# Wider pieces of the experts' weights, a regrouped set of turns, a shorter last routing and a written order at the end, in a hierarchical mixture-of-experts layer

## The chip, the cores and the metric

The kernel runs on 1 core of one Trainium2 chip. The metric is the device time of one execution in microseconds, the median of several runs. A profiled execution is a single one, recorded by the hardware profiler; its span is the time between its first and its last recorded instruction, a little less than the execution's own time.

## The reference, cut to what matters

One layer of a decoder trunk for 1024 tokens of width 1024, in float32. First a mixer (an SSD group, a forgetting attention and a convolution group over one input projection, then one output projection), then a hierarchical mixture of 32 gated-MLP experts of width 512: top-1 of 4 groups, then top-2 of that group's 8 experts. The part that the change is about:

```python
x = x + g_m * y                
h = rms_norm(x, norm_ffn_g[l]) * (1.0 + sc_f) + sh_f
p_g = softmax(h @ w_rg + b_rg); g_sel = argmax(p_g)
e_logits = (h @ w_re + b_re).reshape(m, 4, 8)[g_sel]
top_p, top_i = lax.top_k(softmax(e_logits), 2)
weights = top_p / sum(top_p) * p_gsel
...
hid = silu(xb @ w_gate[e]) * (xb @ w_up[e])
ys = hid @ w_down[e]
out = zeros.at[stok].add(ys[dest] * sw)
x = x + g_f * out
return rms_norm(x, final_norm_g)
```

## The kernel before

**Stages.** The mixer runs first, in eight blocks of 128 tokens; then the output projection with the routing of each block; then the loop over the 32 experts; then the final norm. Float32 accuracy comes from a split: each operand is rounded to a high part (`hi`, made by a copy on ACT) and a remainder (`lo`, made by a subtraction on DVE), and each product is three matmuls, `xh`·`hi`, `xl`·`hi`, `xh`·`lo`.

**Early in the mixer** four tiles of the queries' and keys' weights are worked through by `qk_tile(t)`; inside that loop, after `t == 0`, a small table `ncu` is transposed by PE (L487) and stored.

**Routing.** For each block of 128 tokens, `post_steps` (from L1008) makes the normed tokens `h2` and the router's logits `L`; the logits are made feature-major (`wrp` stationary, `xT` moving), copied by ACT to `rT`, transposed back (L1023) and added up in two operations (L1024, L1025). `h2` of the last block is scaled in one operation over 1024 columns (L1033) and written to `h2_d` in DRAM. `route_steps` (from L1057) makes one-hot rows, positions (L1118 to L1121), the table `tab` of each expert's tokens (matmuls L1131, addition L1135) and from it, in three operations (L1137 to L1139), the integer indices `toki`. `gather(e)` (L1308) is an indirect DMA by GpSimd that fetches the 128 rows of expert `e` from `h2_d` into one of two buffers `xg`, `xq`.

**The experts' weights** are loaded on SP's queue in halves of a matrix (128 x 2048, 1 MB; 6 halves an expert, 192 in all) by `load_half` (issue at L1198). `halves` holds NHALF = 18 buffers, carved by `room` out of the mixer's tiles as these die; 15 are loaded before the routing ends, and POST = 3 are held back and loaded after `gather(0)`, by way of a GpSimd memset behind it. `after_load` lets at most DEPTH = 5 loads run at once (DC = 2 for the first NC_ = 15, DL = 3 for the small ones at the end). `order` is the sequence of the matrices: `(e, 0)` gate, `(e, 1)` up, then `(e-1, 2)` down of the expert before.

**The expert loop.** `xpose(e)` transposes the gathered rows (8 transposes L1318 into two PSUM banks, each split into `xh`, `xl` at L127, L128). `gate_or_up` works through a matrix in four pieces of 1024 columns; `piece` (L1328) casts one on ACT (`phi`) and takes the remainder on DVE (`plo`), three buffers of each. The matmuls (L1340 to L1342) follow in groups of three. `hidden` (L1346 to L1348) is silu on ACT and a product on DVE. `turn_hidden` (4 transposes, L1354) turns it, inside the first matrix of the next expert; `down` (L1368 to L1370) follows `up` of the next expert, and in its middle the tokens of the expert after are transposed and the next gather is issued (`next_tokens`). The result is scaled on DVE (L1374) and scattered with addition into `x1_d` in DRAM (L1378, GpSimd). `row_spread` (L1282) spreads a row of 1024 numbers over the partitions with eight matmuls; it is run for `gf` ahead of the first expert, for `fng` within the last.

**The end.** The eight blocks of `x1_d` are loaded back; `norm_of` (L1292 to L1296) squares a block on ACT, takes the power on GpSimd and scales on DVE. Six blocks (FB) are normed without the last expert's rows, whose 128 tokens are fetched apart into `xr`, added up on GpSimd (L1483), normed and scattered into the output at the end (L1485). For the other two blocks PE adds the last expert's rows with a one-hot matrix (L1470 to L1472).

**The order on each engine** is made by a planner from costs. Instructions that go through `tc.keep_in_program_order` stay in the order in which they are written relative to each other.

The pieces of `gate_or_up` and the step of the loop over the experts read:

```python
            for q in range(4):
                if q == QT and then:
                    then()
                hi, lo = piece(e, m, q)
...
            if e < NE - 1:
                hid = hidden(pg, gate_or_up(e, 1, xh, xl))
                load_next()
                if e:
                    down(e - 1, *hts[e - 1], lambda: next_tokens(e + 1))
```

## Time and profile before

| | us |
|---|---|
| median of 3 runs | 1276.93 (1276.75 to 1277.41) |
| the profiled execution, its own time | 1275.77 |
| its span | 1273.9 |
| PE busy (matmuls) | 1186.6 (93% of the span) |
| PE weight loads busy | 928.3 (73%) |
| DVE busy | 980.5 (77%) |
| ACT busy | 736.4 (58%) |
| GpSimd busy | 268.2 (21%) |
| moved by DMA | 313.21 MB, mean 246 GB/s |

PE, DVE, ACT, POOL and SP are TensorE, VectorE, ScalarE, GpSimd and SyncE; PE's weight loads overlap with its matmuls. A busy share over the whole span is a mean of stages that differ: the loop over the experts takes some 597 of the 1274 us (649.88 to 1246.70), and there the engines stand at other shares than in the mixer before it. The granted clock of PE is a share of full speed (1.00 is 2.4 GHz, 0.50 is 1.2 GHz); its mean over the span is 0.972. A row of the timeline gives the start of an instruction, its duration and, in brackets, for how long its engine had been idle and whose end it waited for; neighbouring instructions of one kind stand in one row, with their number behind the x.

### The profile page before, as it was taken

The numbers are of one execution on the slowest core, as the hardware profiler recorded it, in microseconds if no ns is written. First come the engines' busy times: TensorE is split into PE (matmuls) and PEld (weight loads), VectorE is DVE, ScalarE is ACT, GpSimd is POOL, SyncE is SP. The second block draws the span as 40 slices with busy tenths as digits, with TensorE's granted clock in tenths as the row PEclk, the third lists the DMA queues.
The fourth block names the chain that finished last, engine by engine and source line by source line (L and its number), as shares of the span: only waits on it lengthen the run. The fifth ranks groups of instructions, "written<-read, shape, count | busy, mean of one in ns | idle before, by whom it ended". The sixth has DMA issues, their size and how long they took to land. (4 is left out here: it accounts for less than half of the span.)

```text
span 1273.9 us, 17238 instructions
## 1 busy us (share of the span) xinstructions
PE 1186.6 (93%) x6079; PEld 928.3 (73%) x6079; DVE 980.5 (77%) x1395; ACT 736.4 (58%) x1145; POOL 268.2 (21%) x200
## 2 busy tenths in 40 slices
PE   6999989999999779999779999999999999999993
PEld 4676757868678568778568877777877787787772
DVE  4789992145265676575559999999999999999985
ACT  4323322343354656563258877777877787777763
POOL 3110313100100353432111221122112212211112
PEclk9999999999999989999879999999999999999997
DMA  9316667633201553734889999999999999999726
GB/s 361 140 42 220 210 196 224 160 108 89 78 17 59 148 155 100 262 98 183 304 305 343 361 356 372 366 354 367 369 359 372 356 358 387 363 381 366 236 53 257
DMA packets 93339, 313.21 MB, mean 246 GB/s; under 512 B 23894, under 2 KB 34310, under 8 KB 70976
## 3 DMA queue, kind: packets, MB, share of 16 engines
q1 hardware_dynamic: 60750, 256.25, 54.8%
q10 hardware_dynamic: 14242, 32.51, 7.4%
q0 software_dynamic: 18256, 23.30, 7.2%
q8 instruction: 49, 0.80, 0.3%
q14 instruction: 42, 0.34, 0.1%
HBM read 289.22 MB, written 39.88 MB: 258 GB/s over the span
## 5 line engine op out<-in xcount | busy, mean ns | idle before, releaser
L1342 PE MATMUL ps_gu<-plo,xh 128*128 128x512 f32 x512 | 209.1, 408 | 9.1 <-DVE plo L1328 9.0
L1340 PE MATMUL ps_gu<-phi,xh 128*128 128x512 f32 x512 | 203.3, 397 | 1.4 <-ACT xh L127 1.4
L1328 DVE TENSOR_TENSOR plo<-wx,phi 128x1024 fp32r<-128x1024 f32 x166 | 198.1, 1220 | 7.8 <-ACT phi L1328 5.5
L1328 ACT CAST phi<-wx 128x1024 fp32r<-128x1024 f32 x166 | 173.1, 1054 | 50.7 <-PE ps_gu L1341 40.8
L1341 PE MATMUL ps_gu<-phi,xl 128*128 128x512 f32 x512 | 200.8, 392 | 0.0
L1378 POOL DMA_INDIRECT x_d<-early,toki x31 | 74.9, 2416 | 400.7 <-DVE early L1374 386.0
L1328 ACT CAST phi<-w 128x1024 fp32r<-128x1024 f32 x110 | 115.3, 1050 | 60.4 <-PE ps_gu L1341 53.1
L1328 DVE TENSOR_TENSOR plo<-w,phi 128x1024 fp32r<-128x1024 f32 x110 | 130.7, 1220 | 7.2 <-ACT phi L1328 6.3
L1342 PEld LDWEIGHTS ps_gu<-plo,xh 128*128 128x128 f32 x512 | 96.3, 188 | 40.2 <-DVE plo L1328 20.8
L1340 PEld LDWEIGHTS ps_gu<-phi,xh 128*128 128x128 f32 x512 | 96.5, 189 | 20.2 <-ACT xh L127 1.8
L1341 PEld LDWEIGHTS ps_gu<-phi,xl 128*128 128x128 f32 x512 | 96.5, 188 | 19.6
L1368 PE MATMUL ps_d<-phi,hh 128*128 128x512 f32 x256 | 100.4, 393 | 0.7 <-ACT hh L127 0.7
L1369 PE MATMUL ps_d<-phi,hl 128*128 128x512 f32 x256 | 100.5, 393 | 0.0
L1370 PE MATMUL ps_d<-plo,hh 128*128 128x512 f32 x256 | 96.4, 393 | 0.0
L182 PE MATMUL ps_pr<-h_hi,whi 128*128 128x512 f32 x224 | 91.5, 409 | 0.0
L184 PE MATMUL ps_pr<-h_hi,wlo 128*128 128x512 f32 x224 | 88.8, 396 | 1.3 <-POOL wlo L128 1.3
L183 PE MATMUL ps_pr<-h_lo,whi 128*128 128x512 f32 x224 | 89.2, 398 | 0.0
L225 DVE SCALAR_TENSOR_TENSOR cy<-u_t,cmw,cy 128x1024 f32<-128x1024 f32 x60 | 86.4, 1440 | 2.3 <-ACT cy L222 1.4
L128 POOL TENSOR_TENSOR wlo<-wraw,whi 128x1024 fp32r<-128x1024 f32 x14 | 40.0, 2866 | 161.1 <-ACT whi L127 142.9
L1328 DVE TENSOR_TENSOR plo<-cy,phi 128x1024 fp32r<-128x1024 f32 x44 | 53.8, 1222 | 6.0 <-ACT phi L1328 5.2
L994 PE MATMUL ps_wo<-wo_hi,yh 128*128 128x512 f32 x128 | 55.1, 431 | 2.1 <-ACT yh L127 2.1
L1368 PEld LDWEIGHTS ps_d<-phi,hh 128*128 128x128 f32 x256 | 48.3, 189 | 10.9 <-ACT hh L127 0.9
(405 smaller groups left out, 2570.9 us busy)
## 6 DMA issues: line engine op xcount, KB each, us to landing
w<-in_w_gu_dram SPq DMA_DIRECT2D x54, 1024.0 KB
wx<-in_w_gu_dram SPq DMA_DIRECT2D x50, 1024.0 KB
wx<-in_w_dn_dram SPq DMA_DIRECT2D x30, 1024.0 KB
at<-in_ada_r_dram ACTq DMA_DIRECT2D x64, 256.0 KB
cy<-in_w_gu_dram SPq DMA_DIRECT2D x11, 1024.0 KB
wy<-in_w_gu_dram SPq DMA_DIRECT2D x22, 512.0 KB
wy<-in_w_dn_dram SPq DMA_DIRECT2D x20, 512.0 KB
xq<-in_w_dn_dram SPq DMA_DIRECT2D x10, 1024.0 KB
```

Of the source, the lines that this page charges most:

```text
L182: PE.matmul(ps, hi[:, kt, :], h_hi[hf][:, kt, :], start=(kt == 0), stop=False)
L183: PE.matmul(ps, hi[:, kt, :], h_lo[hf][:, kt, :], start=False, stop=False)
L184: PE.matmul(ps, lo[:, kt, :], h_hi[hf][:, kt, :], start=False, stop=(kt == KT - 1))
L225: yield lambda t=t, k=k: V.scalar_tensor_tensor(cy[:, :, t], v128(u_t[:, t, k:k + T]), cmw[:, t, k:k + 1], cy[:, :, t], op0=ALU.mult, op1= ...
L1328: last[:] = [S.copy(hi, raw).ins, V.tensor_tensor(lo, raw, hi.bitcast(F32), op=ALU.subtract).ins]
L1340: PE.matmul(ps, xh[:, kt], hi[:, ks], start=(kt == 0), stop=False)
L1341: PE.matmul(ps, xl[:, kt], hi[:, ks], start=False, stop=False)
L1342: PE.matmul(ps, xh[:, kt], lo[:, ks], start=False, stop=(kt == KT - 1))
L1368: PE.matmul(pd[n], hh[:, f], hi[:, ns], start=(f == 0), stop=False)
L1369: PE.matmul(pd[n], hl[:, f], hi[:, ns], start=False, stop=False)
L1370: PE.matmul(pd[n], hh[:, f], lo[:, ns], start=False, stop=(f == 3))
L1378: G.indirect_dma_start(x1_d[:, :], bass.IndirectOffsetOnAxis(ap=toki[:, e:e + 1], axis=0), yo[:, :], None, bounds_check=T - 1, oob_is_err= ...
```

## The change

- **Early transpose.** `ncu` is transposed after the second weight tile (`t == 1`) instead of the first, and its place on PE is written.
- **Last routing.** For the last block, 8 matmuls with `xT` stationary make the logits token-major, in one operation on DVE without copy and transpose; `h2` is made and written to DRAM in halves, the second half behind the sum of the one-hot rows. The token numbers are written as `token - T`, and T is added to `tab` early, so that the last addition gives `toki` directly. The operations for the two choices of a token are ordered in pairs.
- **Loads.** NHALF = 17 instead of 18 (the tile `w2` falls away); POST = 6 instead of 3 loads are held, by a dependency on `gather(0)` instead of memsets; NC_ = 11.
- **PE during the first gather.** 25 matmuls on the identity (the ones of the kernel's start) are placed behind `gather(0)`.
- **Pieces.** Casts and remainders are made for 2048 columns at a time (two buffers of each instead of three of half the size). The matmuls of a piece run all on `hi` first, then all on `lo`; all of the experts' matmuls and transposes keep the written order.
- **Turns.** In the middle of `down(e-1)` stand `next_tokens(e+1)` and then `turn_hidden(e)`; expert 1 keeps it inside its first matrix. The turned hidden rows alternate between two tiles. `gf` is spread in the middle of expert 1, `fng` in that of expert 30.
- **Last expert.** `down(30)` and its loads come before the matrices of expert 31.
- **The end** is written out: squares of the six blocks on ACT, four scalings on DVE ahead of the last result, then the split, the addition for `xr` on DVE instead of GpSimd, and the rest; the last two blocks are stored in halves.

The diff, cut:

```diff
-NHALF = 18
+NHALF = 17
-POST = 3
+POST = 6
-QD = 1
-DC, NC_ = 2, 15
+DC, NC_ = 2, 11
-QT = 1
...
-        if t == 0:
+        if t == 1:
-            PE.transpose(pc[:32, 0:P], ncu.rearrange("p h b -> p (h b)"), ident)
+            pin(PE.transpose(pc[:32, 0:P], ncu.rearrange("p h b -> p (h b)"), ident))
...
+            if b == NB - 1:
+                pin(add)
+                pin(V.tensor_tensor(h2[:, qs_], xb[:, qs_], ccn["af"][:, qs_], op=ALU.mult))
...
+            for kt in range(KT):
+                PE.matmul(pr[:, 0:36], xT[:, kt], ccn["wrp"][:, kt, 0:36], start=(kt == 0), stop=(kt == KT - 1))
+            def half_h2(q):
+                hs = slice(512 * q, 512 * (q + 1))
+                pin(V.scalar_tensor_tensor(h2[:, hs], h2[:, hs], s2[:, 3:4], ccn["shf"][:, hs], op0=ALU.mult, op1=ALU.add))
+                S.dma_start(h2_d[bs, hs], h2[:, hs])
+            half_h2(0)
+            pin(V.scalar_tensor_tensor(L[:, b], pr[:, 0:36], s2[:, 3:4], ccn["rbias"], op0=ALU.mult, op1=ALU.add))
...
+        if lastb:
+            pin(so)
+            last_half[0](1)
...
-        if lastb:
-            V.tensor_scalar(tf, tab, 0.0, 8192.0, op0=ALU.is_equal, op1=ALU.mult)
-            V.scalar_tensor_tensor(tf, tab, -1.0, tf, op0=ALU.add, op1=ALU.add)
-            tk.append(V.tensor_copy(toki, tf).ins)
+            tk.append(pin(V.tensor_tensor(toki, pq_[:, 0:NE], tab, op=ALU.add)).ins)
...
-        order += [(e, 0), (e, 1), (e - 1, 2)] if e < NE - 1 else [(e, 0), (e - 1, 2), (e, 1)]
+        order += [(e, 0), (e, 1), (e - 1, 2)] if e < NE - 1 else [(e - 1, 2), (e, 0), (e, 1)]
...
-            room(ew.tile([P, 2048], F32, name="w2"))
...
+            hi = ex.tile([P, 2048], F32R, tag="phi", name="phi", bufs=2)
+            lo = ex.tile([P, 2048], F32R, tag="plo", name="plo", bufs=2)
...
+                for hi, lo, n in pieces(e, m, s):
+                    for k in range(n):
+                        ks = slice(512 * k, 512 * (k + 1))
+                        pin(PE.matmul(ps, xh[:, k0 + k], hi[:, ks], start=(k0 + k == 0), stop=False))
+                        pin(PE.matmul(ps, xl[:, k0 + k], hi[:, ks], start=False, stop=False))
+                    for k in range(n):
+                        ks = slice(512 * k, 512 * (k + 1))
+                        pin(PE.matmul(ps, xh[:, k0 + k], lo[:, ks], start=False, stop=(k0 + k == KT - 1)))
...
         g1 = gather(0)
-        with tc.issue_after(g1.ins):
-            for h in halves[NHALF - POST:]:
-                G.memset(h[0][:, 0:1], 0.0)
+        pw = bank("ps_warm")
+        for _ in range(WARM):
+            pin(PE.matmul(pw[:, 0:P], ident, ident, start=True, stop=True))
         gather(1)
         for _ in range(POST):
-            load_half()
+            load_half(g1.ins)
...
+            def middle():
+                next_tokens(e + 1)
+                turns()
+                if e == 1:
+                    row_spread(gf, sl[0:8, :])
+                if e == NE - 2:
+                    row_spread(fng, early[0:8, D:D + P])
...
+            if e == NE - 1:
                 down(e - 1, *hts[e - 1])
                 load_next()
...
+        sqs = [square(xbs[b]) for b in range(FB)]
+        for b in range(4):
+            finish(b, sqs[b])
+            pin(V.scalar_tensor_tensor(yo_l[:, ns], pd[n], wtab[:, NE - 1:NE], gf[:, ns], op0=ALU.mult, op1=ALU.mult))
+            pin(S.copy(yh[:, ns], yo_l[:, ns]))
+            pin(V.tensor_tensor(yl[:, ns], yo_l[:, ns], yh[:, ns].bitcast(F32), op=ALU.subtract))
+        pin(V.tensor_tensor(xr, xr, yo_l, op=ALU.add))
+        sx = square(xr)
+        for b in range(4, FB):
+            finish(b, sqs[b])
...
```

## Rows read from the trace of the kernel before

**Rows 1.** Timeline of DVE, line L1348: start us, duration us, engine, line, operation
```profile
713.52 0.68 DVE L1348 TENSOR_TENSOR hid<-hid,ps_gu 128x512 f32<-128x512 f32 x1
731.42 0.68 DVE L1348 TENSOR_TENSOR hid<-hid,ps_gu 128x512 f32<-128x512 f32 x1
749.92 0.68 DVE L1348 TENSOR_TENSOR hid<-hid,ps_gu 128x512 f32<-128x512 f32 x1
...
1211.63 0.68 DVE L1348 TENSOR_TENSOR hid<-hid,ps_gu 128x512 f32<-128x512 f32 x1
```

**Rows 2.** Windows, loop: length, then PE, PEld, DVE, ACT, POOL busy; PEclk, DMA share, GB/s
```profile
800.00:900.00 100.00, 98.32 (x456) 79.67 (x455) 96.17 (x98) 78.13 (x90) 17.29 (x10) 1.00 0.99 363
```

**Rows 3.** Timeline of PE, one expert in the loop
```profile
904.53 1.04 PE L1318 MATMUL ps_xg<-ident,xq 128*128 128x128 f32 x8
905.39 0.50 PE L1342 MATMUL ps_gu<-plo,xh 128*128 128x512 f32 x1
...
906.65 0.39 PE L1341 MATMUL ps_gu<-phi,xl 128*128 128x512 f32 x1
907.38 0.50 PE L1342 MATMUL ps_gu<-plo,xh 128*128 128x512 f32 x1 [0.34 <-DVE plo L1328]
...
915.01 0.39 PE L1342 MATMUL ps_gu<-plo,xh 128*128 128x512 f32 x1
```

**Rows 4.** Waits of SP's queue, 780 to 880 us: line, cause, us in total, times, longest
```profile
SPq L1198 <- DVE plo L1328: 78.0, 36, 3.7
```

**Rows 5.** Timeline of SP's queue, two places of the loop
```profile
960.99 8.31 SPq L1198 DMA_DIRECT2D wx<-in_w_gu_dram  x4
...
1018.05 8.63 SPq L1198 DMA_DIRECT2D wx<-in_w_gu_dram  x4
```

**Rows 6.** Timeline of PE, the early transpose
```profile
175.38 0.37 PE L487 MATMUL ps_nc<-ident,ncu 128*32 128x128 f32 x1 [5.27 <-DVE ncu L481]
```

**Rows 7.** Windows, behind the early transpose
```profile
180.00:200.00 20.00, 20.00 (x95) 14.86 (x94) 11.03 (x10) 4.61 (x7) 5.55 (x2) 1.00 0.75 232
```

**Rows 8.** Timeline of DVE and GpSimd, the last routing up to the first gather
```profile
626.30 1.28 DVE L1033 SCALAR_TENSOR_TENSOR h<-h,s,shf 128x1024 f32<-128x1024 f32 x1 [0.44 <-POOL s L124]
...
627.79 0.26 DVE L1025 SCALAR_TENSOR_TENSOR L<-ps_rt,s,L 128x36 f32<-128x36 f32 x1
...
637.46 1.17 POOL L1308 DMA_INDIRECT xg<-h_d,toki  x1 [11.19 <-DMA wx<-in_w_gu_dram]
```

**Rows 9.** The tile `xg`, its 16 gathers and other transfers
```profile
DMA to landing us min/median/max: 3.8/11.9/14.0
```

**Rows 10.** Timeline of PE, from the first gather to the first expert, and the kernel's start
```profile
643.86 3.75 PE L1282 MATMUL ps_row<-sl,ident 8*128 8x128 f32 x16 [5.48 <-DMA sl<-g_rows]
647.54 1.97 PE L1318 MATMUL ps_xg<-ident,xg 128*128 128x128 f32 x8
...
649.88 0.78 PE L1340 MATMUL ps_gu<-phi,xh 128*128 128x512 f32 x1
...
9.64 8.29 PE L292 MATMUL ps_warm<-ident 128*128 128x128 f32 x50 [9.64 <-DVE ident L105]
```

**Rows 11.** Windows, PE's clock ahead of the first expert
```profile
640.00:645.00 5.00, 1.14 (x5) 1.17 (x6) 2.07 (x2) 0.00 (x0) 0.68 (x1) 0.50 0.96 308
```

**Rows 12.** Timeline of DVE, three remainders of 1024 columns in a row
```profile
1220.13 3.49 DVE L1328 TENSOR_TENSOR plo<-w,phi 128x1024 fp32r<-128x1024 f32 x3
```

**Rows 13.** Groups by line and form, DVE, 680 to 1215 us: busy us, mean ns, idle
```profile
L128 DVE TENSOR_TENSOR xl<-ps_xg,xh 128x512 fp32r<-128x512 f32 x60 | 38.5, 683 | 0.0
```

**Rows 14.** Timeline of PE, ACT and DVE, the end
```profile
1246.70 0.39 PE L1370 MATMUL ps_d<-plo,hh 128*128 128x512 f32 x1
...
1251.93 1.06 ACT L1292 ACTIVATE wx<-w 128x1024 f32<-128x1024 f32 x1 [2.01 <-DMA w<-x_d]
...
1264.20 1.28 DVE L1296 SCALAR_TENSOR_TENSOR xg<-xg,s,wx 128x1024 f32<-128x1024 f32 x1 [0.73 <-POOL s L1294]
```

**Rows 15.** Windows, the loads of the kernel's start
```profile
10.00:15.00 5.00, 5.00 (x26) 5.00 (x26) 2.80 (x7) 4.46 (x8) 2.74 (x6) 1.00 1.04 428
```

219 lines of the change are left out of this document (118 added, 101 removed).

## The prediction

> **What bounds the kernel now.** I read four views in this order: the windows by stage, the waits of PE, the timeline of one expert on PE and DVE, and SP's own waits. From 749.92 us to 1211.63 us of the span every expert takes the same time: the line that finishes an expert's hidden row stands in 26 rows there, of which the first and the last are shown, so 461.71 / 25 = 18.47 us each [rows 1]. In that stretch PE and DVE are busy 98 and 96 of 100 us, ACT 78, and the 16 DMA engines 0.99 of the time at 363 GB/s [rows 2]. Three resources stand close together, so the order in which they give out is the question.
>
> PE gives out first. Its own work per expert is 72 matmuls of 512 columns and 12 transposes. Matmuls run at 33 steps in 7.63 us, 0.231 us each (907.38 to 915.01); eight transposes run from 904.53 to 905.39, 0.107 us each [rows 3]. That is 72 x 0.231 + 12 x 0.107 = 16.6 + 1.3 = 17.9 us. The rest, 0.56 us, is a hole in each expert: the step from 906.65 to 907.38 takes 0.73 us instead of 0.23, and the row names the rounding remainder `plo` of DVE as what PE waited for [rows 3]. The early experts have no such hole: there two neighbouring rows stand 17.90 us apart (713.52, 731.42) [rows 1]. So 17.9 us is both worked out and seen.
>
> DMA is next. In the middle of the loop SP waits 78.0 of 100 us for a weight buffer to be freed by DVE [rows 4]: loads are held back by the computation. Later the same 18 half-matrices take longer to issue than three experts take to compute: 960.99 to 1018.05 is 57.06 us, against 3 x 18.47 = 55.4 [rows 5]. There DMA can't keep up, and only the lead in the buffers hides it.
>
> **The change, part by part.**
>
> *The early transpose (L487).* PE sits idle 5.27 us before it, until DVE has made `ncu` [rows 6]. Moved one weight tile later (32 x 3 matmuls, 16 steps of 0.7 us = 11 us), its input is long there. After it PE is busy 20.00 of 20 us while DVE has 9 of 20 free [rows 7], so what was behind the stall moves up and no engine is late in its place. Bounds 0 and -5.3; I take -5.
>
> *Last routing, up to the first gather.* Removed from DVE's chain: a 1.28 us operation at 626.30 in front of the logits becomes one of half the columns, -0.6 (the other half goes behind the one-hot sum, where DVE waits for PE anyway); the second addition of the logits, 0.26 us at 627.79; three operations as small between the table and the integer index, estimated at 0.2 us each; and two groups of operations on the table are interleaved, so that one such wait on a predecessor falls away, 0.3 us by estimate. Together 0.6 + 0.3 + 0.6 + 0.3 = 1.8 us on a chain that ends with the gather's issue at 637.46 [rows 8]. Added: the second half of the last block's tokens is written to DRAM later, from about 632 us, and the gather waits for it; a DMA queued then must land in 3 us. The shortest landing among the gathers into that buffer is 3.8 us after issue [rows 9], so up to 1 us may come back. Bounds 0 and -2.5; I take -1.8: gather at 635.7.
>
> *From the gather to the first expert matmul.* Now 649.88 - 637.46 = 12.4 us. PE first waits 5.48 us for a row queued behind weight loads and spends 3.75 us spreading it over partitions (643.86), then transposes (647.54) [rows 10]. The spread goes into expert 1, where it costs PE its 16 matmuls at twice that rate, +1.9 us. Six half loads are held until the gather has landed, so it has the DMA queues for itself: I take the shortest landing, 3.8 us, against 11.9 in the median [rows 9]. Transposes could start at 635.7 + 3.8 = 639.5. Added are 25 matmuls in front of them; at the kernel's start the same (the row counts 50) took 8.29 us [rows 10]. Behind the last table matmuls at about 636 they end at 644; during the idle stretch of the routing they cost nothing. Transposes therefore start between 639.5 and 644.3, the first expert matmul 0.9 us later. I take 643.0 for that matmul: 7.3 us behind the gather instead of 12.4, -5.1. The clock: it is granted at 0.50 (1.2 GHz) at 640 to 645, where PE is busy 1.14 of 5 us [rows 11], and the first expert's matmuls run slow to 653 us. With PE running through it is 2.4 GHz: the next expert's eight transposes at 1.97 against 1.04 us [rows 3, 10], and some eight matmuls, each at twice 0.231, -0.9 - 8 x 0.2 = -2.5 (bounds 0 and -3.4).
>
> *Pieces of 2048 columns, transposes together.* DVE does one remainder instead of two. Three in a row take 3.49 us [rows 12], so about 1.2 each, and half the size takes 0.683 [rows 13]; merging two 1024s saves between 0 and 2 x 0.683 - 1.22 = 0.15 us, up to 0.9 us an expert on DVE. That does not itself move PE, but it widens the margin whose lack makes the hole. Against it, PE now needs its whole 2048 cast before its first matmul, and only two such buffers exist where three of 1024 did. The pairing (eight matmuls on the cast, four on the remainder) gives DVE 8 x 0.23 = 1.8 us after the first matmul. A cast of 2048 takes about 2 us and a remainder 2.3, and a piece occupies PE 2.77 us, so both engines keep up if the planner orders their queues well. I take the period without the hole, 17.9 us, over the 26 steps that now take 18.47 (the last from 731.42 on): -0.57 x 26 = -14.8; bounds 17.6 (one switch to transposes fewer, 0.1 us, and the steps in strict sequence at 0.228) and 18.46. Fewer buffers (17 halves, not 18) only touch the lead.
>
> *The end.* PE's last expert matmul starts at 1246.70 and DVE's last operation at 1264.20, 17.5 us later [rows 14]. In between DVE does six whole-block scalings of 1.28 us, and ACT waits for blocks of `x1_d` until 1251.93 [rows 14]. With `down` of expert 30 before both matrices of expert 31, its scatter lands some 10 us earlier against the end and the blocks with it; four scalings (4 x 1.2) then fit in front of PE's end, and the addition of the last rows moves from GpSimd to DVE. Against it, the written order makes ACT square all six blocks before it copies the last rows. I take -5, bounds -9 and +3.
>
> Sum against the profiled execution's own 1275.8 us: -5 - 1.8 - 5.1 - 2.5 + 1.9 - 14.8 - 5 = -32.3, so 1243.5. The median of the runs shown is 1.2 us above that execution; I give 1245.
>
> **A rule against it.** At 10 to 15 us the DMA engines moved 428 GB/s [rows 15], so 363 in the loop is not the top that this core can reach. The Trainium skill (HBM Reference, the table at its head and the note under it) gives about 358 GB/s as a core's share when its neighbour streams too, and about 425 alone. By the share the loop would already stand at its ceiling and win nothing; the row at 428 speaks for the other figure.
>
> **Rivals.**
>
> 1. *DMA becomes the bound.* 57.06 us for 18 halves is 3.17 us each [rows 5]. In the new kernel 181 halves (192 less the 17 - 6 loaded before) remain when the gather lands, at 639.5 - 5 = 634.5: 181 x 3.17 = 574, the last at 1208; the last six go in small transfers with three in flight, some 4 us more; cast, remainder and matmuls of the last piece 4, so PE could end at 1216, just ahead of the 1219.6 of the sum (1246.9 - 27.3). The margin is 3 us in 574: at 3.2 us a half it is gone by 2, and the blocks of `x1_d`, queued behind, add some 3; 1250. At 3.23 it would be 1255. For it: the DMA share of 0.99. Against: the rate is that of SP's issues, which the freed buffers set as well. Chance 0.25.
> 2. *The hole stays.* With two large buffers DVE may be late elsewhere, for instance when an `xl` stands behind a 2.3 us remainder. Period 18.4, and all else as summed: 1245 + 26 x 0.5 = 1258. Chance 0.15.
> 3. *Slower.* ACT and DVE run their queues in order. If the cast of the second half of `down` is put behind the three casts of the transposes, PE waits for it in every expert: those casts end about 1.6 us after the last transpose, the cast takes 2 us, so a hole of up to 3 us and a period near 20.5, 32 x 2.6 = +83. It decides from the period at which the other gains (32.3 - 14.8 = 17.5) are used up, 18.47 + 17.5/32 = 19.0 us. At 20.5 the time is 1328, at 19.6 it is 1299. Against it: the planner of the old kernel put such casts ahead. Chance 0.07.
> 4. *The routing and start bring nothing*: the 25 matmuls stand in front of the routing's own, or the gather waits for the late write. 1245 + 6.9 = 1252. Chance 0.08.
>
> The forecast itself, PE-bound with no hole, gets 0.45.
>
> **How the numbers follow.** The likeliest case gives 1245, its own range 1235 to 1255 from the bounds of start and end. The 8 in 10 range takes in rivals 1, 2 and 4 and the lower bound of the period (17.6, -8): 1231 to 1264. A difference under 0.2% (2.6 us) can't be told from none. Faster 0.91, same 0.02, slower 0.07.
>
> **What would show it.** The hidden rows of neighbouring experts 17.9 us apart (18.4 or more: rival 2; over 19.0: rival 3); no wait of PE for `plo`; ACT's casts waiting for weight loads in the last third (rival 1), with PE idle there; the early transpose without a wait; transposes of expert 0 within 9 us of the gather's issue and the clock at 2.4 GHz by then; DVE's last operation 12 to 13 us behind PE's last expert matmul. The prediction is wrong if the period is not between 17.6 and 18.2, or if the loop's weights land after 1215 us.

## The result, and the profile after

The changed kernel takes 1262.82 us (median of 4 runs, 1260.09 to 1264.04) against 1276.84 us before (1275.79 to 1277.41 in the same comparison): a ratio of 0.9888, interval 0.9873 to 0.9902. It is 14.0 us faster, where 32 were forecast. The profiled execution took 1263.57 us with a span of 1261.8 us, 12.1 us shorter than the span before. All terms below are made against that span.

The same marks were read in both traces. Some of the marks before stand in no group ahead: the last block's addition behind the output projection, and the hidden rows of experts 0 to 2 and 31. Timeline of DVE, the kernel before (start, duration, engine, line, operation, in brackets its idle time and what ended it):

```profile
622.88 0.69 DVE L1000 TENSOR_TENSOR xb<-ps_wo,xb 128x512 f32<-128x512 f32 x1 [5.34 <-PE ps_wo L996]
...
664.83 0.68 DVE L1348 TENSOR_TENSOR hid<-hid,ps_gu 128x512 f32<-128x512 f32 x1
677.81 0.68 DVE L1348 TENSOR_TENSOR hid<-hid,ps_gu 128x512 f32<-128x512 f32 x1
695.68 0.68 DVE L1348 TENSOR_TENSOR hid<-hid,ps_gu 128x512 f32<-128x512 f32 x1
...
1237.44 0.68 DVE L1348 TENSOR_TENSOR hid<-hid,ps_gu 128x512 f32<-128x512 f32 x1
```

The same view of the changed kernel, with the last block's addition, then the hidden rows of experts 0 to 2, 5, 30 and 31:

```profile
618.56 0.69 DVE L999 TENSOR_TENSOR xb<-ps_wo,xb 128x512 f32<-128x512 f32 x1 [2.97 <-PE ps_wo L995]
...
653.92 0.68 DVE L1375 TENSOR_TENSOR hid<-hid,ps_gu 128x512 f32<-128x512 f32 x1
667.23 0.68 DVE L1375 TENSOR_TENSOR hid<-hid,ps_gu 128x512 f32<-128x512 f32 x1
689.60 0.68 DVE L1375 TENSOR_TENSOR hid<-hid,ps_gu 128x512 f32<-128x512 f32 x1
...
743.65 0.68 DVE L1375 TENSOR_TENSOR hid<-hid,ps_gu 128x512 f32<-128x512 f32 x1
...
1196.85 0.68 DVE L1375 TENSOR_TENSOR hid<-hid,ps_gu 128x512 f32<-128x512 f32 x1
1224.28 0.69 DVE L1375 TENSOR_TENSOR hid<-hid,ps_gu 128x512 f32<-128x512 f32 x1
```

Each stretch is the difference of two neighbouring marks:

| stretch | before, us | after, us | difference | forecast |
|---|---|---|---|---|
| start to the last block's addition | 622.88 | 618.56 | -4.3 | -5 |
| to the first gather's issue | 14.58 | 13.04 | -1.5 | -1.8 |
| to the first expert matmul | 12.42 | 9.11 | -3.3 | -5.1 |
| to the hidden row of expert 0 | 14.95 | 13.21 | -1.7 | -2.5 |
| expert 0 to 1 | 12.98 | 13.31 | +0.3 | 0 |
| expert 1 to 2 | 17.87 | 22.37 | +4.5 | +1.9 |
| expert 2 to 30 | 515.95 | 507.25 | -8.7 | -14.8 |
| expert 30 to the end of the span | 62.27 | 64.95 | +2.7 | -5 |
| sum | 1273.9 | 1261.8 | -12.1 | -32.3 |

The front brought -10.8 of the -14.4 that were forecast. Most of what is missing lies in three rows: the loop (6.1 us), the end (7.7) and expert 1 (2.6).

**The loop.** Experts 5 to 30 take (1196.85 - 743.65) / 25 = 18.13 us each: better than 18.47 [rows 1], but not 17.9. Timeline of PE in one expert (the last `hi` matmul, the four on the remainder, the next `hi`), then DVE between the transposes and that place:

```profile
971.86 0.39 PE L1365 MATMUL ps_gu<-phi,xl 128*128 128x512 f32 x1
972.36 1.20 PE L1368 MATMUL ps_gu<-plo,xh 128*128 128x512 f32 x4
973.39 0.39 PE L1364 MATMUL ps_gu<-phi,xh 128*128 128x512 f32 x1
```

```profile
966.91 1.28 DVE L126 TENSOR_TENSOR xl<-ps_xg,xh 128x512 fp32r<-128x512 f32 x2
968.11 0.68 DVE L126 TENSOR_TENSOR hx<-ps_ht,hx 128x512 fp32r<-128x512 f32 x1
968.71 1.40 DVE L1411 SCALAR_TENSOR_TENSOR early<-ps_d,wtab,gf 128x512 f32<-128x512 f32 x2
970.02 2.28 DVE L1351 TENSOR_TENSOR plo<-w,phi 128x2048 fp32r<-128x2048 f32 x1
```

PE steps in 0.23 us, so at 972.09 it would have gone on; the remainder ends at 972.3 and PE continues at 972.36, 0.27 us late. DVE had run without a gap since 966.91, and the scaling of the expert before (L1411, 1.40 us), which PE does not wait for, stands ahead of that remainder; `xl` and `hx` do too, but PE needs these first. The waits of the weight loads name the same place 21 times in the 22 experts from 745 to 1150 us (line, cause, total, times, longest):

```profile
PEld ps_gu L1368 <- DVE plo L1351: 9.1, 21, 0.5
```

**The end.** The scatter of expert 30 and the loads of the blocks, GpSimd and SP, the kernel before:

```profile
1231.90 2.29 POOL L1378 DMA_INDIRECT x_d<-early,toki  x1 [11.11 <-DVE early L1374]
```

```profile
1238.75 0.81 SPq L1446 DMA_DIRECT2D wx<-x_d  x2
```

The changed kernel, timelines of GpSimd (the scatters of experts 29 and 30), SP, PE, ACT and DVE:

```profile
1209.32 3.35 POOL L1413 DMA_INDIRECT x_d<-early,toki  x1 [18.33 <-DVE early L1411]
1217.99 3.28 POOL L1413 DMA_INDIRECT x_d<-cy,toki  x1 [5.31 <-DVE plo L1351]
```

```profile
1225.73 4.22 SPq L1487 DMA_DIRECT2D wx<-x_d  x8
```

```profile
1230.69 0.79 PE L1400 MATMUL ps_d<-phi,hx 128*128 128x512 f32 x1 [5.01 <-ACT hx L125]
...
1238.98 0.62 PE L1403 MATMUL ps_d<-plo,hx 128*128 128x512 f32 x2
```

```profile
1229.01 1.06 ACT L1501 ACTIVATE cy<-wx 128x1024 f32<-128x1024 f32 x1 [3.72 <-DMA wx<-x_d]
...
1230.07 0.56 ACT L125 CAST hx<-ps_ht 128x512 fp32r<-128x512 f32 x1
```

```profile
1250.78 2.15 DVE L1549 SCALAR_TENSOR_TENSOR wx<-ps_ad,s,wy 128x512 f32<-128x512 f32 x3
```

The loads wait for the scatter of expert 30, and that one was issued only at 1217.99, 8.7 us behind the scatter of expert 29 into the same tensor, although DVE had its rows ready at 1214.8 (two operations from 1213.43, 1.40 us). The row puts the end of GpSimd's wait down to a remainder of DVE, which the scatter does not use; in eight further profiles the two scatters are likewise 8.5 to 9.1 us apart, and the experiment without the second one, below, shows what is waited for. The loads are asked for 1.45 us behind the last hidden row, where it was 1.31 before: no earlier. So the +2.7 us of this row of the table are 1.6 between the hidden rows of experts 30 and 31 (27.43 for 25.81), 0.1 up to the loads, and 0.9 from the loads to the end (36.07 for 35.15). Besides, ACT squares the first block, which lands at 1229, before it makes the cast `hx` that PE needs: PE stands still for 5.01 us, and its matmuls then take 0.43 us each (1.2 GHz) instead of 0.23.

**Expert 1.** The row that was moved there is spread in 16 matmuls with 8 rows of weights each:

```profile
670.63 1.15 PE L1300 MATMUL ps_row<-sl,ident 8*128 8x128 f32 x8
672.46 1.15 PE L1300 MATMUL ps_row<-sl,ident 8*128 8x128 f32 x8 [0.67 <-ACT gf L1301]
```

The spread keeps PE for 2.9 us (670.63 to 673.54), of which it waits 0.67 for ACT. Behind it the clock falls: it is 0.50 from 674 to 677 us, and the next eight matmuls take 3.29 us, not 8 x 0.23 = 1.8. Windows (length; PE, PEld, DVE, ACT, POOL busy; clock, DMA share, GB/s), first behind the first gather, where [rows 11] had 0.50, then behind the spread, then in the loop, and last behind the same spread in another run (three loads held, below):

```profile
640.00:645.00 5.00, 4.53 (x22) 3.37 (x21) 1.29 (x2) 2.72 (x3) 0.98 (x1) 1.00 1.01 425
672.00:677.00 5.00, 4.54 (x17) 3.73 (x18) 3.69 (x8) 0.99 (x2) 1.61 (x1) 0.69 1.02 416
800.00:900.00 100.00, 99.58 (x467) 80.87 (x466) 94.61 (x72) 74.70 (x61) 34.40 (x12) 1.00 0.98 370
675.00:680.00 5.00, 5.00 (x25) 4.08 (x24) 4.25 (x10) 2.50 (x2) 0.49 (x2) 1.00 0.89 362
```

In that last run the clock stays at 1.00 behind the spread, and expert 1 to 2 takes 20.77 us: 2.9 more than the 17.87 before, the spread alone. The remaining 1.6 of the 4.5 us are the clock.

**The start.** The operation that gives the integer indices `toki`, DVE, the kernel before, then the changed kernel:

```profile
636.98 0.18 DVE L1139 CAST toki<-tf 128x32 int32<-128x32 f32 x1
```

```profile
629.69 0.19 DVE L1157 TENSOR_TENSOR toki<-ps_tab,tab 128x32 int32<-128x32 f32 x1 [0.42 <-PE ps_tab L1150]
```

It ends 14.28 us behind the last block's addition before (637.16) and 11.32 after (629.88): the chain to the indices got 3.0 us shorter. The gather was issued 0.3 us behind it before, and is now issued 1.7 us behind it. GpSimd's first gather, and the warming matmuls and transposes of PE:

```profile
631.60 1.17 POOL L1325 DMA_INDIRECT xg<-h_d,toki  x1 [10.51 <-DMA h_d<-h]
```

```profile
631.84 7.76 PE L1421 MATMUL ps_warm<-ident 128*128 128x128 f32 x48
639.43 1.04 PE L1335 MATMUL ps_xg<-ident,xg 128*128 128x128 f32 x8
640.71 0.49 PE L1364 MATMUL ps_gu<-phi,xh 128*128 128x512 f32 x1 [0.24 <-ACT xh L125]
```

The gather waits for the late half of the tokens, which takes 1.4 of the 3.0 us back. The transposes begin when the 25 matmuls end. The held loads, which wait for this gather to land, are issued from 635.92 us on, so its rows were there 4.3 us behind its issue, and 3.5 us before the transposes.

### The profile page after: what moved, and what is told of

The parts are those of the page before. It is cut to its first block, busy times and chain, and to the rows that moved or that the text cites. A ratio compares the mean times of both kernels' runs of the same rounds, so it can differ in the third digit from the quotient of the medians.

```text
span 1261.8 us, 16662 instructions
## 1 busy us (share of the span) xinstructions
PE 1191.5 (94%) x6128; PEld 938.4 (74%) x6128; DVE 959.9 (76%) x1219; ACT 709.8 (56%) x976; POOL 337.0 (27%) x204
## 4 chain that ended last, share of the span: by engine, by line
PE 73%; DVE 9%; DMA 7%; issue 4%; ACT 4%; POOL 2%; SPq 0%; POOLq 0%; ACTq 0%; DVEq 0%
PE ps_gu L1368 8%; PE ps_gu L1365 7%; PE ps_gu L1364 7%; DVE plo L1351 4%; PE ps_pr L180 4%; PE ps_d L1400 4%; PE ps_d L1401 4%; PE ps_pr L181 4%; PE ps_pr L182 4%; PE ps_d L1403 4%; PE ps_o L599 3%; PE ps_wo L993 2%; PE ps_wo L994 2%; PE ps_wo L995 2%; PE ps_xg L1335 1%
## 5 line engine op out<-in xcount | busy, mean ns | idle before, releaser
L1351 DVE TENSOR_TENSOR plo<-wx,phi 128x2048 fp32r<-128x2048 f32 x88 | 199.6, 2289 | 15.2 <-ACT phi L1351 15.1
L1351 ACT CAST phi<-wx 128x2048 fp32r<-128x2048 f32 x88 | 168.0, 1909 | 71.6 <-PE ps_gu L1365 40.0
L1368 PE MATMUL ps_gu<-plo,xh 128*128 128x512 f32 x512 | 142.7, 396 | 1.3
L1351 DVE TENSOR_TENSOR plo<-w,phi 128x2048 fp32r<-128x2048 f32 (+1 forms) x48 | 107.3, 2245 | 12.1 <-ACT phi L1351 12.0
L1368 PEld LDWEIGHTS ps_gu<-plo,xh 128*128 128x128 f32 x512 | 94.1, 188 | 30.0 <-DVE plo L1351 11.5
L1365 PEld LDWEIGHTS ps_gu<-phi,xl 128*128 128x128 f32 x512 | 96.2, 188 | 25.0 <-DVE xl L126 3.5
L1351 ACT CAST phi<-w 128x2048 fp32r<-128x2048 f32 (+1 forms) x48 | 89.7, 1872 | 41.3 <-PE ps_gu L1365 23.0
L1400 PE MATMUL ps_d<-phi,hx 128*128 128x512 f32 x256 | 106.3, 415 | 5.0 <-ACT hx L125 5.0
L1401 PE MATMUL ps_d<-phi,hx 128*128 128x512 f32 x256 | 103.4, 404 | 0.0
L126 POOL TENSOR_TENSOR wlo<-wraw,whi 128x1024 fp32r<-128x1024 f32 x14 | 39.9, 2855 | 158.1 <-ACT whi L125 139.7
L1325 POOL DMA_INDIRECT xq<-h_d,toki x16 | 41.7, 2608 | 142.4 <-PE ps_xg L1335 123.7
L1325 POOL DMA_INDIRECT xg<-h_d,toki x16 | 38.6, 2414 | 152.0 <-PE ps_xg L1335 80.3
L1403 PE MATMUL ps_d<-plo,hx 128*128 128x512 f32 x256 | 72.1, 398 | 0.0
L1400 PEld LDWEIGHTS ps_d<-phi,hx 128*128 128x128 f32 x256 | 49.9, 195 | 15.7 <-ACT hx L125 5.2
## 6 DMA issues: line engine op xcount, KB each, us to landing
w<-in_w_gu_dram SPq DMA_DIRECT2D x29, 1024.0 KB, 10.3
```

The source lines that it names most:

```text
L1351: last[:] = [S.copy(hi[:, cs], raw).ins, V.tensor_tensor(lo[:, cs], raw, hi[:, cs].bitcast(F32), op=ALU.subtract).ins]
L1365: pin(PE.matmul(ps, xl[:, k0 + k], hi[:, ks], start=False, stop=False))
L1368: pin(PE.matmul(ps, xh[:, k0 + k], lo[:, ks], start=False, stop=(k0 + k == KT - 1)))
L1400: pin(PE.matmul(pd[n], hh[:, f], hi[:, ns], start=(f == 0), stop=False))
L1401: pin(PE.matmul(pd[n], hl[:, f], hi[:, ns], start=False, stop=False))
L1403: pin(PE.matmul(pd[n], hh[:, f], lo[:, ns], start=False, stop=(f == 3)))
```

## The experiments

All are edits of the changed kernel, some on top of one another, but for one of the kernel before. A ratio is always against the kernel before on the same chip; the changed kernel stands at 0.9888.

### The loop: the order on DVE

The scaling of an expert's result and its scatter are put behind the remainders that PE needs next, for all but the last experts:

```diff
+                pcs = pieces(e, m, s)
+                if s and late_:
+                    with tc.issue_after(last[1]):
+                        late_()
...
-                down(e - 1, *hts[e - 1], middle)
+                res = down(e - 1, *hts[e - 1], middle)
```

> The changed kernel, but the two scalings of an expert's result on DVE (and its scatter) stand behind the remainder of the second half of the next gate matrix, not ahead of it. Theory A (order of DVE's queue: that remainder is late by 0.27 us in each expert because xl, xl, hx and the two scalings, 3.4 us, stand ahead of it): the period falls from 18.13 to 17.9 us and the time by 5 to 7 us. Theory B (DVE has 17.8 us of work in an expert, as much as PE, so the lateness only moves to another piece): period 18.05 or more, less than 2 us. Theory C (DMA delivers a half matrix each 3.02 us and no faster): period 18.1, PE and ACT now wait for loads.

1255.93 us, ratio 0.9831 (0.9815 to 0.9848), 6.9 us less than the changed kernel. The period from expert 5 to 28 is (1153.26 - 741.99) / 23 = 17.88 us; the waits for the remainder at L1368's place fall from 21 to 3. The hole was the order on DVE, not its load. The last two steps stay at 19.26 and 18.88 us.

Is it the DMA engines that hold those two? The same without the scatters of experts 0 to 28, whose results are then missing in the output:

```diff
+                if e >= NE - 3:
+                    G.indirect_dma_start(x1_d[:, :], bass.IndirectOffsetOnAxis(ap=toki[:, e:e + 1], axis=0), yo[:, :], None,
+                                         bounds_check=T - 1, oob_is_err=False, compute_op=ALU.add)
```

> The kernel of early_late without the scatters of the experts 0 to 28 into x1_d: their results are left out of the output, and some 1 MB of the 7.5 MB that DMA moves for an expert with them. Theory A (DMA is the bound near the end of the loop: in early_late two experts there take 19.3 and 18.9 us): these two take 17.8 to 18.0 us like the others, and SP again waits for buffers in the second half. Theory B (the two are late for another reason, in DVE's or PE's order): they stay at 19 us.

1257.56 us in a single execution. Those steps are 19.26 and 18.90 us, though the DMA share fell from 0.97 to 0.88 in the one and from 0.68 to 0.16 in the other. With the scatters SP waits for earlier loads to land in much of 850 to 950 us; without them its only wait is for buffers that DVE frees:

```profile
SPq L1217 <- DVE plo L1351: 85.8, 38, 4.2
```

PE's time is the same in both, so transfers do not set these steps: rival 1 does not hold here. In both steps DVE waits 0.9 us for a cast of ACT that stands behind those of the transposes, and ahead of these ACT is idle for 1.78 and 2.36 us. That is the order that rival 3 described, at 1.0 to 1.4 us an expert; no run moves this cast alone, so that it is the cause is not shown.

Then the size of the pieces: 1024 columns again, four buffers of each, but PE's written order, turns and all else as changed.

```diff
-            hi = ex.tile([P, 2048], F32R, tag="phi", name="phi", bufs=2)
-            lo = ex.tile([P, 2048], F32R, tag="plo", name="plo", bufs=2)
...
+            for raw in wts[e, m][s][0:2]:
+                hi = ex.tile([P, 1024], F32R, tag="phi", name="phi", bufs=4)
+                lo = ex.tile([P, 1024], F32R, tag="plo", name="plo", bufs=4)
```

> The changed kernel with casts and remainders of 1024 columns again, in four buffers of each in the place of two of 2048; a piece's matmuls still run on the cast first, then on the remainder, and all else is as changed. Theory A (the wide pieces brought the period from 18.47 to 18.13 us): the period goes back to 18.4 us and the time rises by 5 to 8 us. Theory B (the written order of PE and the turns together brought it; with half the size DVE can go on sooner and one remainder is late less): period 17.9 to 18.0 us, the time falls by 3 to 6 us.

1259.23 us, ratio 0.9858 (0.9841 to 0.9876): not slower than with wide pieces. Twenty experts in a row take 17.75 us each (725.84 to 1080.91), less than with 2048 columns. One reading is that DVE's small operations fit between shorter remainders; that was only argued. One step near the end takes 23.06 us. Timelines of DVE and PE there:

```profile
1163.10 1.41 DVE L1408 SCALAR_TENSOR_TENSOR early<-ps_d,wtab,gf 128x512 f32<-128x512 f32 x2 [2.86 <-DMA x_d<-early,toki]
```

```profile
1165.69 0.73 PE L1365 MATMUL ps_gu<-plo,xh 128*128 128x512 f32 x2 [3.27 <-DVE plo L1347]
```

DVE may not overwrite the only result buffer `early` before the scatter of the expert before has landed; behind it in DVE's queue stands the remainder that PE wants. That scatter's issue alone kept GpSimd busy for 10.27 us (from 1143.32), where the one after it takes 2.32. With a second buffer for results (and three of `plo`, which makes room for it) that must go:

```diff
-            yo = free[1] if e == NE - 2 else early[:, 0:D]
+            yo = free[1] if e == NE - 2 else yo2_ if e % 2 else early[:, 0:D]
```

> The kernel of small_pieces with two buffers in turn for the scaled result that is scattered (three buffers of 1024 for the remainders instead of four, to make room). In small_pieces 22 steps of the loop took 17.81 us each and one near its end 23.1, in which DVE's scaling waited 2.9 us for the scatter before it to leave the only buffer. Theory A (that buffer is the cause): the long step falls to 17.8 to 18.5 us, the time to 1253 to 1255. Theory B (the loads of weights have fallen behind by then and the lateness only shows there): a step of 21 us or more stays near the end.

1253.29 us, ratio 0.9832 (0.9810 to 0.9854). The long step is gone; the last five are 18.2 to 18.5 us. So the loop's gain does not come from the wide pieces, which took part of it back. What else the change made there (PE's written order, casts before remainders, the turns), and one more buffer for casts than before, were not told apart.

### The start

The early transpose alone, in the kernel before:

```diff
-        if t == 0:
+        if t == 1:
             pc = bank("ps_nc")
-            PE.transpose(pc[:32, 0:P], ncu.rearrange("p h b -> p (h b)"), ident)
+            tc.keep_in_program_order(PE.transpose(pc[:32, 0:P], ncu.rearrange("p h b -> p (h b)"), ident))
```

> The kernel before, with the early transpose moved behind the second weight tile and its place on PE written, and nothing else of the change. Theory A: the stretches behind it move up by 4.4 us, as they stand in the changed kernel's trace (addition of the last block at 622.9 becomes 618.5), and all of it reaches the end: 1272.5. Theory B: it is given back, since the expert loop waits for weights whose loads start no earlier: under 1 us.

1271.32 us, ratio 0.9954 (0.9937 to 0.9970): -5.5 us. The last block's addition stands at 618.29, -4.6, and the whole keeps it. This term was right, alone as in the sum.

Then `gf` spread ahead of the loop again, as in the kernel before:

```diff
-    row_load(g_rows[0, 3072:4096], sl[0:8, :])
+    row_load(g_rows[0, 3072:4096], early[0:8, 0:P]); row_spread(gf, early[0:8, 0:P])
...
-                if e == 1:
-                    row_spread(gf, sl[0:8, :])
```

> The changed kernel, but the row gf is loaded into an early buffer and spread over the partitions by PE before the first gather, not in the middle of expert 1. Theory A (the spread costs PE its 2.9 us in the loop and brings the clock down to 1.2 GHz for the matmuls behind it): the hidden rows of experts 1 and 2 stand 18.1 us apart instead of 22.4, and the time falls by 4 us (about 1259). Theory B (expert 2 is late because the casts and remainders of the turns stand together on ACT and DVE, not because of the spread): the distance stays above 21 us and the time moves by less than 1 us.

1262.94 us, ratio 0.9893 (0.9877 to 0.9910). Expert 1 to 2 takes 18.09 us instead of 22.37: the spread cost 4.3 us there. But nothing is won: the hidden row of expert 0 comes 39.9 us behind the last block's addition (657.29 - 617.35) instead of 35.4, since the spread now stands in PE's queue ahead of the warming matmuls, and these are all done before the transposes may start. Timeline of PE:

```profile
631.14 3.35 PE L1300 MATMUL ps_row<-early,ident 8*128 8x128 f32 x14
634.42 8.55 PE L1421 MATMUL ps_warm<-ident 128*128 128x128 f32 x50
642.81 1.04 PE L1335 MATMUL ps_xg<-ident,xg 128*128 128x128 f32 x8
```

Ten warming matmuls instead of 25, and then none (the loop is left out):

```diff
-        for _ in range(WARM):
+        for _ in range(10):
             pin(PE.matmul(pw[:, 0:P], ident, ident, start=True, stop=True))
```

> The changed kernel with 10 matmuls on the identity behind the first gather instead of 25. In the changed kernel the 25 end at 639.4 us, while the gather, issued at 631.6, lands 4.3 us later, at 635.9. Theory A (the 25 hold the first transposes back): transposes start at 635.9 to 636.3, the first hidden row 3.3 us earlier, the time 3 us less (about 1260). Theory B (what is won at the start is lost to loads, which start no earlier): first hidden row 3.3 us earlier, the end less than 1 us.

> The changed kernel without the matmuls on the identity behind the first gather. Theory A (they keep PE's clock up): transposes start at 635.9 us, but they and the first matmuls run at 1.2 GHz as in the kernel before, which takes 2.5 us back; against the changed kernel -1 us at the first hidden row. Theory B (the clock would be up by then anyway): -3.4 us there, as with 10.

With ten, 1260.83 us, ratio 0.9889 (0.9855 to 0.9924); with none, 1261.35 us, ratio 0.9878 (0.9850 to 0.9907). Against the whole time that is nothing one can tell. Against the last block's addition, the hidden row of expert 0 comes at 35.36 us with 25, at 32.34 (649.32 - 616.98) with 10 and at 36.39 (652.72 - 616.33) with none. The transposes, first with ten, then with none:

```profile
634.80 1.06 PE L1335 MATMUL ps_xg<-ident,xg 128*128 128x128 f32 x8 [1.05 <-DMA xg<-h_d,toki]
```

```profile
636.26 1.97 PE L1335 MATMUL ps_xg<-ident,xg 128*128 128x128 f32 x8 [6.64 <-DMA xg<-h_d,toki]
```

With ten they wait for the rows, 4.60 us behind the gather's issue, at 2.4 GHz (1.06 us for eight); with none they run at 1.2 GHz (1.97) and start 6.36 us behind it. Of the 4.1 us between ten and none, 1.9 lie behind the start of the transposes (14.52 and 16.46 us to the hidden row): that is the clock. Most of the rest lies ahead of it, where with none the gather's own issue takes GpSimd 3.20 us, against 1.17 with ten and with 25:

```profile
629.90 3.20 POOL L1325 DMA_INDIRECT xg<-h_d,toki  x1 [11.04 <-DVE wtab L1190]
```

No run shows whether the missing matmuls have to do with that. So by the clock, warming is worth 1.9 us, and the other 15 matmuls cost 3.0.

Three loads held instead of six:

```diff
-POST = 6
+POST = 3
```

> The changed kernel with three loads held until the first gather has landed, not six. Theory A (the gather's 4.3 us are owed to the empty queues; with three loads of 1 MB in flight it lands some 8 us after its issue, at 639.6, about where the 25 matmuls end): first hidden row 0 to 1 us later, time within 1 us. Theory B (the gather then takes the median of 11.9 us): first hidden row 4 us later, time +4 us. Theory C (loads that start earlier serve the loop): time 1 to 3 us less.

1263.49 us, ratio 0.9904 (0.9881 to 0.9927), not told apart from six. The place of the cost was another than expected: the transposes start 4.5 us after the gather's issue, so it lands no later, but it is issued 17.97 us behind the last block's addition instead of 13.04. The indices are ready as early as in the changed kernel (11.3 us behind it), but the tokens' late half, whose write is asked for at 625.70, has landed only by 634.2, where a cast of ACT that waits for it starts; in the changed kernel it is 627.19 and 630.8. With fewer loads held, its write takes 8.5 us instead of 3.6. The gather (its row puts the wait down to a load):

```profile
635.04 1.17 POOL L1325 DMA_INDIRECT xg<-h_d,toki  x1 [15.45 <-DMA wx<-in_w_gu_dram]
```

### The end

The cast `hx` of the last expert ahead of the squares on ACT:

```diff
-        sqs = [square(xbs[b]) for b in range(FB)]
+        with tc.issue_after(hxc[-1]): sqs = [square(xbs[b]) for b in range(FB)]
```

> The changed kernel, but ACT makes the cast of the last turned hidden row (hx) ahead of the first square of the end instead of behind it. In the changed kernel PE stands idle 5.0 us there, and its matmuls behind run at 1.2 GHz. Theory A (ACT's queue order is what makes the end late): PE's idle goes to about 0.7 us, its last expert matmul comes 5 to 7 us earlier, and the whole takes 4 to 7 us less than the changed kernel (about 1257). Theory B (the end hangs on the blocks of x1_d, whose loads start when the scatter of expert 30 has landed; the last two squares wait for them at 1240 and stand ahead of the split of the last result): PE's end moves by the same 5 to 7 us, but the squares of the last two blocks stay where they are and the whole changes by less than 1 us.

1263.79 us, ratio 0.9892 (0.9875 to 0.9908): nothing. PE waits 0.68 us for `hx` instead of 5.01, and its last expert matmul is at 1235.0, though the last hidden row came 1.5 us later than in the changed kernel. The span ends 34.6 us behind the issue of the block loads, against 36.1 in the changed kernel and 35.2 before. PE's stall, striking as it is, cost 1.5 us at most: the blocks' landing sets the end. In the changed kernel the chain that ended last holds 12.13 us for these loads, from 1229.12.

The squares in another order too (four, then the last rows, then two), and in a second version the result ahead of three of the four early scalings on DVE:

```diff
+        sqs += [square(xbs[b]) for b in range(4, FB)]
         pin(V.tensor_tensor(xr, xr, yo_l, op=ALU.add))
         sx = square(xr)
```

```diff
-        for b in range(4):
-            finish(b, sqs[b])
+        finish(0, sqs[0])
...
-        for b in range(4, FB):
+        for b in range(1, FB):
             finish(b, sqs[b])
```

> The changed kernel; at the end ACT casts the last turned hidden row first (as in end_order), and squares the two blocks that land last behind the split of the last result, not ahead of it. Theory A (the end hangs on those two blocks, which land at 1240 us: as long as their squares stand ahead of the split of the last result, nothing behind PE's last matmul can start): PE's earlier end now counts, the matmuls that add the last rows start 4 us earlier, the time falls by 4 to 6 us (about 1258). Theory B (the blocks of the last two groups are needed for these matmuls just as late): less than 1.5 us.

> The changed kernel with the cast of the last turned hidden row first on ACT, and on DVE only one block's scaling ahead of the last expert's result (not four); three squares stand ahead of the split on ACT, the others and the five other scalings behind. In end_squares PE's last expert matmul ended at 1234.0 us, but the result's scaling came at 1240.1, behind four block scalings that came 2.05 us apart, each behind two GpSimd operations on a column. Theory A (the four scalings ahead of the result are the bound of the end): the result's scaling starts within 1 us of PE's last expert matmul, DVE's last operation comes 4 to 5 us earlier against the last hidden row, the time is 1257 to 1259. Theory B (DVE has 14 us of work behind PE's end, whatever its order, and the blocks land late): less than 2 us.

1262.60 us (0.9880, 0.9860 to 0.9899) and 1261.29 us (0.9885, 0.9868 to 0.9902). In the first, the block scalings come 2.05 us apart, because the small operation of GpSimd between square and scaling takes 1.0 to 1.2 us while DVE scales; timeline of GpSimd, the first and the fourth, and of DVE, the scaling beside the fourth:

```profile
1231.79 0.25 POOL L1502 TENSOR_SCALAR s<-s 128x1 f32<-128x1 f32 x1 [2.80 <-ACT cy L1501]
...
1237.03 1.17 POOL L1502 TENSOR_SCALAR s<-s 128x1 f32<-128x1 f32 x1 [0.23 <-ACT cy L1501]
```

```profile
1236.84 1.28 DVE L1507 SCALAR_TENSOR_TENSOR wx<-wx,s,wy 128x1024 f32<-128x1024 f32 x1 [0.77 <-POOL s L1503]
```

GpSimd's operation ends at 1238.20, 0.08 us behind the scaling (1238.12), and the two before it likewise (0.09 and 0.08): it does not run slower, it ends when DVE has ended. So each scaling holds up the number that the next one needs.

In the second the result is scaled at 1232.71, at PE's end, and then the fifth block has not landed (its square starts at 1239.88). The end stands 33.5 us behind the loads instead of 36.1; the median is 1.5 us less than with the changed kernel, within the intervals.

`fng` spread behind the last turn instead of in expert 30:

```diff
-                if e == NE - 2:
-                    row_spread(fng, early[0:8, D:D + P])
...
+        hx31 = turn_hidden(NE - 1, hid); row_spread(fng, early[0:8, D:D + P]); pd = down(NE - 1, *hx31)
```

> The changed kernel, but fng is spread behind the turn of expert 31's hidden row, where PE stands idle for 5 us, and not in the middle of down of expert 29. Theory A (as with gf, the spread takes 2.9 us of PE and leaves the matmuls behind it at 1.2 GHz; it also delays the scatter of expert 29, which holds back that of expert 30, and this the loads of the blocks): the last hidden row comes 5 us earlier and the end 4 to 5 us (about 1258). Theory B (the last loads of weights are the bound by then): the last hidden row comes less than 2 us earlier, the time changes by less than 2 us.

1261.00 us, ratio 0.9866 (0.9845 to 0.9886). The median is 1.8 us less, within the intervals. In the profiled execution the loads are issued 2.0 us earlier (1223.74) and the span ends 2.1 us earlier. The step from expert 30 to 31 takes 23.93 us instead of 27.43, so the second spread cost 3.5 us there: 2.0 by itself, since in three runs that keep it the clock stays at 1.00 behind it and the step takes 25.9, and 1.5 by the clock. Against that, expert 22 to 23, which the edit does not touch, takes 20.01 us instead of 18.15. There a scatter's issue kept GpSimd for 7.79 us instead of 3.38, and DVE had to wait for the only result buffer. Six of the ten profiles that share this loop have that long issue, and a step of 18.9 to 20.0 us.

Now the scatter itself; that of expert 30 is not made:

```diff
-            G.indirect_dma_start(x1_d[:, :], bass.IndirectOffsetOnAxis(ap=toki[:, e:e + 1], axis=0), yo[:, :], None,
+            if e < NE - 2: G.indirect_dma_start(x1_d[:, :], bass.IndirectOffsetOnAxis(ap=toki[:, e:e + 1], axis=0), yo[:, :], None,
```

> The changed kernel without the scatter of expert 30's result into x1_d; that part of the output is left out. In the changed kernel this scatter is issued at 1218.0 us, after the one of expert 29 (1209.3) has landed, and lands at 1225.7, where the loads of the blocks start; in nine runs the end of the span stands 33.5 to 37.6 us behind that point. Theory A (the scatter's landing sets the end): the loads start at about 1218 us, the squares stop holding back the last expert, and the end comes 5 to 8 us earlier (1255 to 1258). Theory B (PE's last matmuls and what follows them set it): loads earlier, end within 2 us (1261 to 1263).

1257.99 us, ratio 0.9864 (0.9848 to 0.9881); in its own comparison the kernel before took 1275.71 us, so 17.7 us below it, against 14.0. The loads are issued 7.9 us behind the issue of the scatter of expert 29 (1209.02 us), when it has landed, with the last hidden row where it was (1223.99 us):

```profile
1216.89 3.69 SPq L1487 DMA_DIRECT2D wx<-x_d  x8
```

The span is 1255.5 us, 6.3 us shorter, of the 8.8 us by which the loads are earlier; then DVE and PE are last. So the chain at the end of the changed kernel is: scatter 29, scatter 30, loads, squares, scalings.

### Together

The late result scaling, early `gf`, six warming matmuls, late `fng` and the squares; then with the result ahead of the scalings; then that with 1024 columns and two result buffers. New in it is only

```diff
-        for _ in range(WARM):
+        for _ in range(6):
```

> The changed kernel with gf spread before the first gather in the place of most of the matmuls on the identity (6 of 25 stay), the scalings of a result behind the next remainder (early_late), fng spread late, and the squares of the end as in end_squares. Theory A (the parts add up: -4 for gf, -3 for the start, -7 for the scalings, -4 to -9 for the end): 1239 to 1245. Theory B (in the second half of the loop the loads wait for each other and no longer for buffers; what the experts gain is given back as waits for weights towards the end of the loop, and only the end's gain counts beside early_late's): 1247 to 1252, with experts of 19 us and more near the end of the loop.

> The kernel of combined with the order of the end as in end_yo_first. Theory A (DVE's order bounds the end there too; the result's scaling came 1.3 us behind PE's end in combined): 2 to 4 us less than combined, 1247 to 1249. Theory B (nothing): 1250 to 1252.

> The kernel of combined_2 with pieces of 1024 columns (four buffers for the casts, three for the remainders) and two buffers for the scattered result. Theory A (with the order on DVE settled, 17.8 us, PE's own work, is the period to the end of the loop): 5 us less than combined_2, 1242 to 1244. Theory B (the loads are the bound: last hidden rows no earlier than in combined_2): 1247 to 1249, with PE waiting near the end of the loop.

1251.35 us (0.9798, 0.9782 to 0.9814), 1252.09 us (0.9805, 0.9784 to 0.9826) and 1247.02 us (0.9761, 0.9742 to 0.9779). The first two miss the sum of their parts: the loop's last steps stay at 19.4 and 18.9 us, and with six warming matmuls, behind the spread, the transposes start at 1.2 GHz again (1.72 and 1.92 us for eight). The third is the best kernel of this study, 16 us better than the change. Its loop keeps 17.77 us to the end; window of it, and the hidden rows of experts 5 and 30:

```profile
800.00:900.00 100.00, 100.00 (x473) 83.19 (x473) 99.03 (x102) 81.45 (x90) 19.57 (x11) 1.00 0.97 364
```

```profile
737.17 0.69 DVE L1376 TENSOR_TENSOR hid<-hid,ps_gu 128x512 f32<-128x512 f32 x1
...
1181.50 0.69 DVE L1376 TENSOR_TENSOR hid<-hid,ps_gu 128x512 f32<-128x512 f32 x1 [0.36 <-PE ps_gu L1369]
```

PE is busy all of 100 us, DVE 99.

## Why the prediction was wrong in size and right in direction

- **What bounds the kernel: right, but DMA is closer than its margin says.** PE's own work was worked out as 17.9 us an expert; the best kernel shows 17.77 with PE never idle. The rival of a DMA bound was priced by SP's issues, 3.17 us a half, which "the freed buffers set as well". They did so in part: in those 57 us SP waits 16.3 us for buffers and 33 for earlier loads. In the best kernel it hardly waits for buffers any more (903 to 1135 us: line, cause, total, times, longest):

```profile
SPq L1217 <- DVE plo L1347: 2.5, 9, 0.3
```

  It issues a half every 3.10 us there (75 halves from 903.06 to 1135.24), while PE uses one every 2.96. So what the prediction says of the kernel before holds for the best one too: DMA does not keep up, and the lead in the buffers hides it to the end. The Trainium skill (HBM Reference, Specifications) gives about 358 GB/s as a core's share beside a streaming neighbour; the 425 at 640 to 645 us speaks for the other figure, as the row at 428 did. The 364 in the loop, with the DMA engines busy for 0.97 of the time, lies near the first; why the loop gets no more, no run shows.
- **Early transpose: right** (-4.3 us; alone -5.5). The "32 x 3" matmuls of a weight tile are a slip, the 16 steps of three beside it are right; nothing was added up from it.
- **Last routing, -1.5 for -1.8: right in the sum by luck.** The chain to the indices got 3.0 us shorter, not 1.8, and the wait for the late half of the tokens took 1.4 back, where the prediction allowed up to 1 and took nothing. It was not run alone.
- **Gather to first matmul, -3.3 for -5.1: the warming matmuls were mis-sized.** The prediction had both ends, the rows' landing and the end of the 25 matmuls, and took a value between them. The transposes stand behind the 25 in PE's queue, so the later end alone counts: 7.8 us behind the gather's issue (631.60 to 639.43), where 6.4 was taken. With ten PE is at 2.4 GHz too, and they end before the rows land.
- **`gf` spread, +4.5 for +1.9: the failed step is "16 matmuls at twice that rate".** By itself the spread cost 2.9 us, 0.67 of them a wait for ACT between its halves; the clock behind it, which was put at nothing, cost 1.6 in this execution. The second spread, of `fng`, was not counted at all, and costs 2.0 by itself and 1.5 by the clock.
- **The loop, -8.7 for -14.8: the step that failed is "both engines keep up if the planner orders their queues well".** It was a condition, and nothing in the trace of before supported it. The mechanism named as rival 2, a hole of PE behind DVE's queue, was right, at half its price: 18.13, not 18.4. Not an `xl` but the scaling of a finished result stood in the way. That the wide pieces widen the margin was of little use: DVE's busy time in 100 us went from 96.2 to 94.6, and narrow pieces with the same order of PE gave 17.75. The prediction's own signs were too wide to show this failure: 18.13 lies between 17.6 and 18.2, and the last weights were asked for by 1196.4 us. What did show it is the sign "no wait of PE for `plo`".
- **The end, +2.7 for -5: the failed step is "its scatter lands some 10 us earlier".** Against the last hidden row, expert 30's rows were ready 3.9 us earlier than the old scatter's issue (1224.28 - 1214.83 against 1237.44 - 1231.90), not 10. Of these 3.2 went to the wait for the scatter of expert 29 and 1.0 to GpSimd's issue (3.28 us instead of 2.29), so the loads start no earlier against that row. The hidden rows of 30 and 31 moved apart by 1.6 us, where the `fng` spread now is. The forecast that DVE would end 12 to 13 us behind PE's last expert matmul held (13.0), but that says little when DVE waits for the landing and PE has been stalled by it. The order of squares before `hx` was seen and priced in the bounds; it showed as 5 us on PE and cost 1.5 at most.

Of the 20 us that are missing, the runs account for most one by one: the spreads 2.6 more than priced and 2 to 3.5, the order on DVE 6.9, the chain of scatters 4 to 6, fifteen warming matmuls 3. They do not add up in one kernel without the narrow pieces. Executions of one changed kernel lie several us apart (1260.09 to 1264.04 here), so that differences of 2 us stay within the intervals. The profiles show two places where they part: the clock behind each spread, which stays at 1.00, or is low for some 3 us (+1.6) or 6 us (+3.2; expert 1 to 2 takes 23.96 us with the late scaling), and the long issue of one scatter (+0.8 to +1.9). What decides between these is open.

## What to carry to other kernels

A period worked out from one engine's instructions is a floor; whether it is reached is decided by the order in the queue of the next engine, so look there for work that nobody waits for, ahead of work that somebody does. A transfer that is started earlier is worth what the last link of its chain allows, so follow it back through every transfer into the same memory before pricing it. And an eye-catching stall (5 us of PE) is worth nothing until it is shown that the end moves with it: price it by the engine or transfer that is last, not by its length.
